# A two-layer HGRN2 and forgetting-attention trunk on one core: meta tokens turned first, a second PSUM bank for a head's outputs, half-tile parts stacked, key tiles that end with query tiles

## The chip, the core and the metric

The kernel runs on one NeuronCore of a Trainium2 chip. Its engines are TensorE (PE in the profile; PEld is its weight loads), VectorE (DVE), ScalarE (ACT), GpSimd (POOL) and SyncE (SP, which issues the DMAs). Each runs its own instructions in order and waits for others by semaphores. The metric is the device time of one execution in microseconds (us); lower is better.

## The reference

A sequence of 16 meta tokens and 1024 real ones, 1024 features wide, goes through two layers. The first mixes by a gated linear recurrence, the second by forgetting attention; each is followed by a feed-forward net with a causal convolution of width 3.

```python
# layer 0: per head (8 heads, 128 wide), chunks of 64 tokens, the meta tokens one chunk of 16
S_t = diag(f_t) S_{t-1} + k_t v_t^T ;  o_t = S_t^T q_t
o = RMSNorm_per_head(o) * head_gain * silu(g) ;  mix = o @ w_out
# layer 1: per head (16 heads, 64 wide), causal, one shared k, v and decay sum c
p = softmax(q k^T / 8 + c_q - c_k) ;  o = p @ v ;  mix = o @ w_out
# after each: h += RMSNorm(mix), then
u = causal_conv3(RMSNorm(h) @ w_up)          # 2 x 2752 columns
h += RMSNorm((silu(gate) * val) @ w_down)    # 2752 rows
```

## The kernel before

Features lie on partitions, tokens on the free axis, in three blocks of 342 or 356 tokens. Matrix products are made from operands split in a high and a low part: `mm3s` (L137) issues three matmuls for each 128 rows of contraction, wh by xh (L141), wh by xl (L142) and wl by xh (L143). Weights come by `Weights.cols` and `Weights.rows`: a DMA into a raw tile, ACT's cast into wh, DVE's subtraction into wl (`split`, L96). PSUM tiles have tags with a fixed number of buffers: pj 2, g 3, pd 2, po 1.

*FFN* (`ffn`, L591). 2752 hidden features are 21 tiles of 128 and one half tile of 64. `tile_up` makes a tile's hidden values hh and hl. `downs` adds a chunk of three or four tiles into 8 accumulators, three blocks each. The half tile is in the first chunk, with two full ones: its high and low parts lie in two tiles, 64 rows each, and its three matmuls contract 64 rows.

*Recurrence* (`recurrence`, L438). For each head it turns values and key parts by PE transposes (`turn`, L448: two groups of four 128x128 blocks, then the meta tokens at L457, whose 16 rows ACT copies into mt), makes the scores, the start state from the meta tokens (L490), the state products (L496) and the outputs (L516, L518), four blocks per PSUM tile po, which ACT evacuates twice, copy and square (L505, L506). `weave` (L248) mixes this stream on PE with the next head's input projections by columns yielded, and PE's order there is written out by that, not by the scheduler.

*Attention* (L750 on). Queries go in tiles of 114, three to a block. `score_steps` makes a query tile's logits and softmax in a tile L, of a width kn that ends with the query tile. `sum_steps` turns L in key tiles of 128 (L899), copies each into pTh and pTl, and adds v by pTh (L911) and v by pTl (L912) into po. The keys are 1040 wide, so the last key tile, which only the third block of a head reads, has 16 rows. The values are turned to key rows by `turn` (L789), in three steps per head pair: 2, 3 and 3 key tiles and the tail of 16, each copied by ACT (L805, L809) and subtracted by DVE (L806, L810). POOL clears the part of L between kn and the end of its key tile (L864). `weave` mixes the heads with the next pairs' projections. Outside of these two woven stretches a scheduler orders all engines.

Of the kernel before, what the change touches and what calls it, by code (L numbers as in the profile page):

```python
# [12 lines left out]
U32 = mybir.dt.uint32  # L13
# [42 lines left out]
def tile_yoco(ctx: ExitStack, tc: tile.TileContext, hT, gains, lbl, w_in, head_g, w_oa,  # L56
# [23 lines left out]
    def f(ap):  # L80
        return ap.bitcast(F32)
# [18 lines left out]
    class Weights:  # L100
# [28 lines left out]
            return lambda kt: (wh[:, kt * P:(kt + 1) * P], wl[:, kt * P:(kt + 1) * P])  # L129

        def rows(self, w, r0, n=P, name="w"):
            raw, wh, wl = self.load(lambda raw: [(raw[:n, :D], w[r0:r0 + n, :])], name)
            with tc.high_priority(offset=self.offset):
                split(wh[:n, :D], wl[:n, :D], raw[:n, :D])
            return lambda ot: (wh[:n, ot * P:(ot + 1) * P], wl[:n, ot * P:(ot + 1) * P])

    def mm3s(pt, pairs, sl):  # L137

        n = len(pairs)
        for j, ((wh, wl), (xh, xl)) in enumerate(pairs):  # L140
            PE.matmul(pt, wh, xh[:, sl], start=(j == 0), stop=False)  # L141
            PE.matmul(pt, wh, xl[:, sl], start=False, stop=False)  # L142
            PE.matmul(pt, wl, xh[:, sl], start=False, stop=(j == n - 1))  # L143
            yield 3 * pt.shape[-1]

    def mm3(pt, pairs, sl):
        for _ in mm3s(pt, pairs, sl):
# [290 lines left out]
    def recurrence(h):  # L438
# [8 lines left out]

        def turn(src, dst, j):  # L448

            for b4 in range(2):  # L450
                pt = psum("g")
                for j4 in range(4):
                    PE.transpose(pt[:, j4 * P:(j4 + 1) * P], src[:, pr(4 * b4 + j4)], ident)
                A.copy(dst[:, 4 * b4:4 * b4 + 4].rearrange("p j v -> p (j v)"), pt)
                yield 8 * P
            pm = psum("g")
            PE.transpose(pm[:, :P], src[:, :P], ident)  # L457
            A.copy(mt[:NMETA, j], pm[:NMETA, :P])
            yield 2 * P


        decay = sm.tile([P, 3, NPAIR], F32, tag="decay", name=nm("decay"))
# [47 lines left out]
        evacuate(slice(0, NMETA), pm[:, :NMETA])  # L510
        yield 4 * NMETA
        for b4 in range(2):
            po = psum("po")
            for j in range(4 * b4, 4 * b4 + 4):
                oc = slice(j % 4 * P, (j % 4 + 1) * P)
                PE.matmul(po[:, oc], vt[:, j], atv[:, j], start=True, stop=False)  # L516
                yield 4 * P
                PE.matmul(po[:, oc], S[:, j], qi[:, pr(j)], start=False, stop=True)  # L518
                yield 4 * P
            evacuate(slice(NMETA + 512 * b4, NMETA + 512 * b4 + 512), po)  # L520
# [70 lines left out]
    def ffn(l, blocks, x, r, WW, hid, accu, done, then=None):  # L591
# [21 lines left out]

        def tile_up(j):
            c0, m = HID[j]
            hh, hl = (unit(i, f"h{j}", F32R) for i in hid[count["hid"] % len(hid)])
            count["hid"] += 1
            ws = [WW.cols(w_up[l], [c0]), WW.cols(w_up[l], [DFF + c0])] if m == P else [WW.cols(w_up[l], [c0, DFF + c0])]
            halo = [None, None]

            def block(t0, n):
                sl, y = slice(t0, t0 + n), []
                for i, w in enumerate(ws):
                    if i:
                        yield
                    pt = psum("pj")[:, :n]
                    mm3(pt, [(w(kt), x[kt]) for kt in range(KT)], sl)
                    with tc.high_priority(offset=OFF):
                        yi, halo[i] = conv(pt, j + i * FT, halo[i], sl)
                    y.append(yi)  # L630
                if m < P:
                    y.append(tmp("y", n))
                    A.copy(y[1][:m], y[0][m:2 * m])
                yg, yv = y[0][:m], y[1][:m]
                A.activation(yg, yg, AF.Silu)
                V.tensor_mul(yv, yv, yg)
                split(hh[:m, sl], hl[:m, sl], yv)
                yield

            return (hh[:m], hl[:m]), block  # L640

        def first(b):
            if not ups:
# [109 lines left out]
    NG = 2 * KT * NB  # L753
    lo, hi = slice(0, HD), slice(HD, P)
    WA = Weights([30, 31], [(37, 41), (42, 43), (39, 44)])
    pair = [dict() for _ in range(KT)]
    head_ = [dict() for _ in range(2 * KT)]
    seen = set()
# [30 lines left out]
    def turn(hp, i):  # L789

        p = pair[hp]
        if i == 0:
            p["vs"] = [unit(VS[hp % 2][j], f"vs{j}", F32R)[:, :D].rearrange("p (k c) -> p k c", c=P) for j in range(2)]
            p["tail"] = tmp("res", 2 * P, F32R)[:NMETA].rearrange("p (k c) -> p k c", c=P)
        ks = [(0, 1), (2, 3, 4), (5, 6, 7)][i]
        vT = p["v"][1]
        pt = psum("g")
        for j, k in enumerate(ks):
            PE.transpose(pt[:, j * P:(j + 1) * P], vT[:, k * P:(k + 1) * P], ident)
        if i == 2:  # L800
            PE.transpose(pt[:NMETA, 3 * P:], vT[:, SEQ:], ident)
        p3 = pt.rearrange("p (k c) -> p k c", c=HD)
        for j in range(2):
            d, q = p["vs"][j][:, ks[0]:ks[-1] + 1], p3[:, j:2 * len(ks):2]
            A.copy(d[:, :, :HD], q)  # L805
            V.tensor_sub(d[:, :, HD:], q, f(d[:, :, :HD]))  # L806
        if i == 2:
            d, q = p["tail"], p3[:NMETA, 6:]
            A.copy(d[:, :, :HD], q)  # L809
            V.tensor_sub(d[:, :, HD:], q, f(d[:, :, :HD]))  # L810
        seen.add(("turn", hp, i))

    def halves(n, i):
# [20 lines left out]
    def dense():  # L834
        for hp in range(1, KT):
            for i in range(NB):
                yield from project("v", hp, i)
                if i:
                    turn(hp, i - 1)
                    yield 3 * P  # L840
            for i in range(NB):
                yield from project("k", hp, i)
                if i == 0:
                    turn(hp, 2)
                    yield 4 * P
                yield from project("q", hp, i)
        while ("split", 2 * KT - 1, NB - 1) not in seen:
            yield None
        yield from one()

    def score_steps(s):


        n, g = divmod(s, NB)
        h, g0 = head_[n], BLK_B[g][0]
        out = h[g] = []
        for i in range(3):
            q0 = g0 + i * QT
            kn = q0 + QT
            L = unit(rot("p", PU), "L")  # L860
            c4 = sm.tile([P, 8], F32, tag="c4", name=nm("c4"), bufs=4)[:QT]
            pad = min(T, -(-kn // P) * P)
            if pad > kn:
                G.memset(L[:QT, kn:pad], 0.0)  # L864
            pcs = pieces(kn)
            for x, (a, b) in enumerate(pcs):
                pt = psum("pd")[:QT, :b - a]
                last = x == len(pcs) - 1
                PE.matmul(pt, h["q"][0][:, q0:q0 + QT], h["k"][:, a:b], start=True, stop=False)
                PE.matmul(pt, h["q"][1][:, q0:q0 + QT], h["k"][:, a:b], start=False, stop=not last)  # L870
                if last:
                    PE.matmul(pt[:, b - a - QT:], identb[:QT], maskb[:QT], start=False, stop=True)
                with tc.high_priority(offset=OFF):
                    V.tensor_tensor_reduce(L[:QT, a:b], pt, h["c"][:QT, a:b], 1.0, 3e38 if x == 0 else c4[:, x - 1:x],
                                           ALU.add, ALU.min, c4[:, x:x + 1])
                if last:
                    A.activation(L[:QT, :kn], L[:QT, :kn], AF.Exp, scale=-1.0, bias=c4[:, x:x + 1], accum_out=c4[:, 5:6])
                    V.reciprocal(c4[:, 6:7], c4[:, 5:6])
                    V.tensor_scalar(L[:QT, :kn], L[:QT, :kn], c4[:, 6:7], None, ALU.mult)
                    out.append((L, kn))  # L880
                yield 2 * (b - a) + last * QT

    def sum_steps(s):
# [2 lines left out]
        g0, gn = BLK_B[g]  # L886
        pu = head_[n][g]
        p, j = pair[n // 2], n % 2
        nk = -(-pu[-1][1] // P)
        av = psum("po")  # L890
        pT = {}

        def turned(kt):
            c0 = rot("pt", [0, gn, 2 * gn])
            kw = min(P, T - kt * P)
            f0 = min(i for i in range(3) if kt * P < pu[i][1])
            pt = psum("g")
            for i in range(f0, 3):
                PE.transpose(pt[:kw, i * QT:(i + 1) * QT], pu[i][0][:QT, kt * P:kt * P + kw], ident[:QT, :QT])  # L899
# [7 lines left out]

        def summed(kt):
            th, tl, ts = pT[kt]
            v = p["vs"][j][:, kt] if th.shape[0] == P else p["tail"][:, j]  # L910
# [57 lines left out]
            yield SLACK  # L968

    def list_steps(s):  # L970
        nk = -(-(BLK_B[s % NB][0] + 3 * QT) // P)
        return sum_steps(s), 4 * 3 * QT * nk

    o_last = []
    B0 = BLK_B[0][0]
# [91 lines left out]
```

## Time and profile before

| | |
|---|---|
| median of 3 runs | 2924.54 us (2918.55 to 2925.66) |
| profiled execution | 2919.62 us, span 2917.9 us |
| PE busy | 2796.7 us, 96% |
| DVE, ACT, POOL busy | 1819.5, 1258.1, 389.8 us |
| moved by DMA | 162.64 MB, 56 GB/s on average |

Busy is the time in which an engine has an instruction under way; for PE the ends of matmuls are modelled and overlap, so the starts in a timeline say more. The waits of PEld show when the next weight load could have begun and did not.

### The profile page before, as it was taken

The page shows a single profiled execution, that of the slowest core. Times are in us where ns is not written, and L with a number is a line of the kernel's source. Part 1 is how long each engine was busy: PE and PEld are TensorE (multiplying, and loading weights), DVE is VectorE, ACT ScalarE, POOL GpSimd, SP SyncE. Part 2 cuts the span into 40 slices and gives each one's busy share as a digit, 9 for nine tenths or more (in the row PEclk, how much of TensorE's full clock was granted, in tenths as well). Part 3 has the DMA queues.
Part 4 walks back from the last instruction along what each step waited for, and adds up shares of the span by engine and source line. Part 5 has one row for each costly group of instructions (what it writes and reads, how often), then busy time and mean ns, then how long its engine had stood idle before and what let it go on. Part 6 is the DMA issues. An engine that isn't in the chain of part 4 may idle for free. (4 is left out here: it accounts for less than half of the span.)

```text
span 2917.9 us, 45973 instructions
## 1 busy us (share of the span) xinstructions
PE 2796.7 (96%) x17754; PEld 2711.2 (93%) x17754; DVE 1819.5 (62%) x3713; ACT 1258.1 (43%) x2399; POOL 389.8 (13%) x851
## 2 busy tenths in 40 slices
PE   8999999999999999999799999998989999999997
PEld 8899999888999999999789898898988999999997
DVE  5545444276555655656878888887683655565566
ACT  6444445445322322323466666666564322232232
POOL 2000000042000100103511111100140100010012
PEclk9999999999999999999899999999999999999999
DMA  4111111132111111111311111112241111111103
GB/s 131 29 37 30 37 37 44 44 102 78 51 44 37 52 51 51 44 51 45 107 49 44 45 45 45 45 44 94 66 122 58 44 51 44 37 53 49 51 30 111
DMA packets 202763, 162.64 MB, mean 56 GB/s; under 512 B 13952, under 2 KB 194096, under 8 KB 202544
## 3 DMA queue, kind: packets, MB, share of 16 engines
q1 hardware_dynamic: 202544, 159.70, 18.7%
q8 instruction: 139, 2.28, 0.3%
q14 instruction: 80, 0.66, 0.1%
HBM read 139.01 MB, written 20.66 MB: 55 GB/s over the span
## 5 line engine op out<-in xcount | busy, mean ns | idle before, releaser
L141 PE MATMUL pj<-x,wh 128*128 128x342 f32 (+1 forms) x2640 | 871.3, 330 | 11.8 <-DVE z L731 6.1
L143 PE MATMUL pj<-x,wl 128*128 128x342 f32 (+1 forms) x2640 | 848.8, 321 | 1.7 <-DVE wl L98 1.7
L142 PE MATMUL pj<-x,wh 128*128 128x342 f32 (+1 forms) x2640 | 848.5, 321 | 0.0
L141 PEld LDWEIGHTS pj<-x,wh 128*128 128x128 f32 x2640 | 500.4, 190 | 19.0 <-ACT sq L181 5.9
L143 PEld LDWEIGHTS pj<-x,wl 128*128 128x128 f32 x2640 | 499.3, 189 | 2.0 <-DVE wl L98 2.0
L142 PEld LDWEIGHTS pj<-x,wh 128*128 128x128 f32 x2640 | 500.8, 190 | 0.2
L97 ACT CAST wh<-raw 128x1024 fp32r<-128x1024 f32 (+1 forms) x202 | 208.5, 1044 | 348.4 <-PE g L142 281.9
L141 PE MATMUL g<-h,wh 128*128 128x342 f32 (+2 forms) x1056 | 347.5, 331 | 0.1
L98 DVE TENSOR_TENSOR wl<-raw,wh 128x1024 fp32r<-128x1024 f32 (+1 forms) x202 | 255.8, 1274 | 141.8 <-ACT wh L97 116.9
L142 PE MATMUL g<-h,wh 128*128 128x342 f32 (+2 forms) x1056 | 338.9, 322 | 0.0
L143 PE MATMUL g<-h,wl 128*128 128x342 f32 (+2 forms) x1056 | 338.0, 321 | 0.0
L141 PE MATMUL pj<-hnh,wh 128*128 128x356 f32 (+1 forms) x720 | 261.6, 363 | 9.6 <-ACT wh L97 7.3
L669 DVE TENSOR_TENSOR acc<-acc,g 128x342 f32<-128x342 f32 (+1 forms) x288 | 147.2, 512 | 193.6 <-PE g L143 193.4
L143 PE MATMUL pj<-hnh,wl 128*128 128x356 f32 (+1 forms) x720 | 233.2, 324 | 0.8 <-DVE wl L98 0.8
L142 PE MATMUL pj<-hnl,wh 128*128 128x356 f32 (+1 forms) x720 | 232.9, 323 | 0.0
L606 ACT ACTIVATE y<-u,cw 128x342 f32<-128x342 f32 (+1 forms) x258 | 150.6, 584 | 181.2 <-DVE u L601 173.6
L607 DVE SCALAR_TENSOR_TENSOR y<-u,cw,y 128x342 f32<-128x342 f32 (+1 forms) x258 | 149.5, 579 | 114.5 <-ACT y L606 114.3
L141 PEld LDWEIGHTS g<-h,wh 128*128 128x128 f32 (+1 forms) x1056 | 198.4, 189 | 20.4 <-issue 18.7
L182 POOL TENSOR_TENSOR acc<-acc,sq 128x342 f32<-128x342 f32 (+1 forms) x162 | 170.9, 1061 | 302.5 <-ACT sq L181 272.3
L601 DVE TENSOR_TENSOR u<-pj,r 128x342 f32<-128x342 f32 (+1 forms) x258 | 132.6, 514 | 118.2 <-PE pj L143 113.8
L142 PEld LDWEIGHTS g<-h,wh 128*128 128x128 f32 (+1 forms) x1056 | 199.5, 189 | 1.3 <-issue 0.8
L143 PEld LDWEIGHTS g<-h,wl 128*128 128x128 f32 (+1 forms) x1056 | 199.3, 189 | 0.4 <-issue 0.4
(231 smaller groups left out, 4804.5 us busy)
## 6 DMA issues: line engine op xcount, KB each, us to landing
raw<-in_w_up_dram SPq DMA_DIRECT2D x84, 512.0 KB, 4.0
raw<-in_w_dn_dram SPq DMA_DIRECT2D x42, 512.0 KB, 4.5
raw<-in_w_in_dram SPq DMA_DIRECT2D x32, 512.0 KB, 4.1
raw<-in_kv_w_dram SPq DMA_DIRECT2D x16, 512.0 KB, 4.1
res<-h SPq DMA_DIRECT2D x44, 171.0 KB, 2.7
h<-mix SPq DMA_DIRECT2D x40, 171.0 KB, 2.1
cn<-csum SPq DMA_DIRECT2D x32, 171.0 KB, 3.7
raw<-in_w_oa_dram SPq DMA_DIRECT2D x8, 512.0 KB, 3.5
```

The source lines that it names most:

```text
L97: A.copy(hi, src)
L98: V.tensor_sub(lo, src, f(hi))
L141: PE.matmul(pt, wh, xh[:, sl], start=(j == 0), stop=False)
L142: PE.matmul(pt, wh, xl[:, sl], start=False, stop=False)
L143: PE.matmul(pt, wl, xh[:, sl], start=False, stop=(j == n - 1))
L182: eng.tensor_add(acc, acc, sq)
L601: V.tensor_mul(u[:, 2:], pt, r()[:, sl])
L606: A.activation(y, u[:, 2:], AF.Copy, scale=cw[:, j, 2:3])
L607: V.scalar_tensor_tensor(y, u[:, 1:n + 1], cw[:, j, 1:2], y, ALU.mult, ALU.add)
L669: V.tensor_add(acc_u[ot][:, sl], acc_u[ot][:, sl], pt)
```

## The change

Four edits. (1) The half tile's high and low parts lie under each other in one tile of 128 rows; its rows of w_down are loaded twice, one copy under the other, and the lower half of wl is cleared on POOL. `mm3s` then issues two matmuls for it instead of three. (2) `turn` of the recurrence turns the meta tokens before the two groups of blocks. (3) The second half of a head's outputs takes a PSUM tile of tag g instead of po. (4) Key tile 0 has 128 keys, the other eight 114, so that they end where query tiles end; the tile L is no longer cleared, the values are turned to the same tiles (rows 114 to 127 of the first tile by a copy and a subtraction of their own, since the others have 114), and the tail becomes a tile of 114 rows.

```diff
@@ Weights.rows
-            raw, wh, wl = self.load(lambda raw: [(raw[:n, :D], w[r0:r0 + n, :])], name)
+            raw, wh, wl = self.load(lambda raw: [(raw[i:i + n, :D], w[r0:r0 + n, :]) for i in range(0, P, n)], name)
...
-                split(wh[:n, :D], wl[:n, :D], raw[:n, :D])
...
+                A.copy(wh[:, :D], raw[:, :D])
+                if n < P:
+                    G.memset(wl[n:, :D].bitcast(U32), 0)
+                V.tensor_sub(wl[:n, :D], raw[:n, :D], f(wh[:n, :D]))
@@ mm3s
-            PE.matmul(pt, wh, xl[:, sl], start=False, stop=False)
+            if xl is not None:
+                PE.matmul(pt, wh, xl[:, sl], start=False, stop=False)
@@ recurrence
+            pm = psum("g")
+            PE.transpose(pm[:, :P], src[:, :P], ident)
+            A.copy(mt[:NMETA, j], pm[:NMETA, :P])
+            yield 2 * P
             for b4 in range(2):
...
-            pm = psum("g")
-            PE.transpose(pm[:, :P], src[:, :P], ident)
-            A.copy(mt[:NMETA, j], pm[:NMETA, :P])
-            yield 2 * P
...
-            po = psum("po")
+            po = psum(("po", "g")[b4])
@@ ffn, block
-                split(hh[:m, sl], hl[:m, sl], yv)
+                if m == P:
+                    split(hh[:, sl], hl[:, sl], yv)
+                else:
+                    A.copy(hh[:m, sl], yv)
+                    V.tensor_sub(hh[m:, sl], yv, f(hh[:m, sl]))
@@ attention
+    KEYS = [(0, BLK_B[0][0] + QT)] + [(BLK_B[0][0] + k * QT, QT) for k in range(1, NQ)]
...
         for j in range(2):
...
+            parts = [(p["vs"][j][:QT, 3 * i:3 * i + n], p3[:QT, j:2 * n:2])]
+            if i == 0:
+                parts.append((p["vs"][j][96:, :1], p3[96:, j:j + 1]))
+            elif i == 2:
+                parts.append((p["tail"][:QT, j:j + 1], p3[:QT, 4 + j:5 + j]))
+            for d, q in parts:
+                A.copy(d[:, :, :HD], q)
+                V.tensor_sub(d[:, :, HD:], q, f(d[:, :, :HD]))
...
-                    yield 3 * P
+                    yield 6 * P
...
-                    yield 4 * P
+                    yield 6 * P
...
-            if pad > kn:
-                G.memset(L[:QT, kn:pad], 0.0)
...
-        nk = -(-pu[-1][1] // P)
+        nk = 3 * g + 3
...
-            kw = min(P, T - kt * P)
-            f0 = min(i for i in range(3) if kt * P < pu[i][1])
+            k0, kw = KEYS[kt]
+            f0 = max(0, kt - 3 * g)
```

In PE's order before, one group of the first down projection of layer 0: g is the PSUM tile; h_733 and h_734, h_741 and h_742 are the high and low parts of the two full tiles, h_749 and h_750 those of the half tile.

```order
L141 MATMUL g_6268<-h_733_5420,wh_6137 128x342
L142 MATMUL g_6268<-h_734_5421,wh_6137 128x342
L143 MATMUL g_6268<-h_733_5420,wl_6138 128x342
L141 MATMUL g_6268<-h_741_5434,wh_6143 128x342
L142 MATMUL g_6268<-h_742_5435,wh_6143 128x342
L143 MATMUL g_6268<-h_741_5434,wl_6144 128x342
L141 MATMUL g_6268<-h_749_5448,wh_6149 128x342
L142 MATMUL g_6268<-h_750_5449,wh_6149 128x342
L143 MATMUL g_6268<-h_749_5448,wl_6150 128x342
```

The same group in PE's order now (L145, L148 and L149 are the former L141, L142 and L143):

```order
L145 MATMUL g_6269<-h_733_5420,wh_6136 128x342
L148 MATMUL g_6269<-h_734_5421,wh_6136 128x342
L149 MATMUL g_6269<-h_733_5420,wl_6137 128x342
L145 MATMUL g_6269<-h_741_5434,wh_6142 128x342
L148 MATMUL g_6269<-h_742_5435,wh_6142 128x342
L149 MATMUL g_6269<-h_741_5434,wl_6143 128x342
L145 MATMUL g_6269<-h_749_5448,wh_6148 128x342
L149 MATMUL g_6269<-h_749_5448,wl_6149 128x342
```

The half tile has two matmuls instead of three, and h_750 is gone.

In PE's order before, the recurrence of the second head where its key parts are turned: d is what is turned, mt holds the meta tokens' turned rows, and hnh, hnl, wh, wl belong to the woven projection of the next head.

```order
L453 MATMUL g_1352<-ident,d_932 128x128 x4
L141 MATMUL pj_1324<-hnh_15_94,wh_1213 128x342
L142 MATMUL pj_1324<-hnl_16_95,wh_1213 128x342
L143 MATMUL pj_1324<-hnh_15_94,wl_1214 128x342
L141 MATMUL pj_1380<-hnh_1_80,wh_1375 128x356
L142 MATMUL pj_1380<-hnl_2_81,wh_1375 128x356
L143 MATMUL pj_1380<-hnh_1_80,wl_1376 128x356
L457 MATMUL g_1384<-ident,d_932 128x128
L490 MATMUL g_1387<-mt 128x128
```

The same place now (L463 is the former L453, L496 the former L490):

```order
L463 MATMUL g_1346<-ident,d_932 128x128 x4
L145 MATMUL pj_1324<-hnh_13_92,wh_1213 128x342
L148 MATMUL pj_1324<-hnl_14_93,wh_1213 128x342
L149 MATMUL pj_1324<-hnh_13_92,wl_1214 128x342
L145 MATMUL pj_1324<-hnh_15_94,wh_1213 128x342
L148 MATMUL pj_1324<-hnl_16_95,wh_1213 128x342
L149 MATMUL pj_1324<-hnh_15_94,wl_1214 128x342
L463 MATMUL g_1358<-ident,d_932 128x128 x4
L145 MATMUL pj_1383<-hnh_1_80,wh_1378 128x356
L148 MATMUL pj_1383<-hnl_2_81,wh_1378 128x356
L149 MATMUL pj_1383<-hnh_1_80,wl_1379 128x356
L496 MATMUL g_1387<-mt 128x128
```

The meta tokens' transpose has moved ahead of these rows, and three dense matmuls stand between the last turned blocks and the reader of mt.

In ACT's order before, the same place of the third head: kt is the copy of four turned blocks, mt that of the meta tokens.

```order
L454 COPY kt_1726<-g_1843 128x512
L454 COPY kt_1726<-g_1855 128x512
L97 CAST wh_2128<-raw_2127 128x1024
L361 ACTIVATE s_1776<-s_1776 128x342
L458 COPY mt<-g_1887 16x128
```

And now (L464 is the former L454, L367 the former L361):

```order
L458 COPY mt<-g_1843 16x128
L464 COPY kt_1726<-g_1849 128x512
L97 CAST wh_2128<-raw_2127 128x1024
L464 COPY kt_1726<-g_1861 128x512
L367 ACTIVATE s_1776<-s_1776 128x342
```

The copy of mt now stands first, and the second copy of kt has come to stand behind the weight cast.

## Rows read from the trace of the kernel before

**Rows 1.** The page, part 1: busy time, share of the span, instructions.

```profile
PE 2796.7 (96%) x17754; PEld 2711.2 (93%) x17754; DVE 1819.5 (62%) x3713; ACT 1258.1 (43%) x2399; POOL 389.8 (13%) x851
```

**Rows 2.** Windows: stretch, its us, busy PE PEld DVE ACT POOL (count), clock, DMA.

```profile
702.58:746.15 43.57, 43.57 (x218) 33.23 (x216) 5.74 (x12) 15.16 (x33) 0.85 (x4) 1.00 0.09 25
1490.00:2076.00 586.00, 561.02 (x3738) 526.28 (x3738) 474.79 (x1324) 368.64 (x891) 48.62 (x124) 0.99 0.17 48
```

**Rows 3.** Timeline of PE, down projection: start, duration, line, out<-in, rows*columns.

```profile
704.33 0.42 PE L141 MATMUL g<-h,wh 128*128 128x342 f32 x1
704.59 0.32 PE L142 MATMUL g<-h,wh 128*128 128x342 f32 x1
...
705.22 0.32 PE L143 MATMUL g<-h,wl 128*128 128x342 f32 x1
705.47 0.42 PE L141 MATMUL g<-h,wh 64*128 64x342 f32 x1
705.73 0.32 PE L142 MATMUL g<-h,wh 64*128 64x342 f32 x1
705.88 0.32 PE L143 MATMUL g<-h,wl 64*128 64x342 f32 x1
706.13 0.43 PE L141 MATMUL g<-h,wh 128*128 128x342 f32 x1
```

**Rows 4.** Line L336, a clear on POOL: ns min/median/max, starts, form.

```profile
L336 POOL MEMSET at<- x1: 968/968/968, 1.7 to 1.7; 128x1040 f32 x1
```

**Rows 5.** Waits of PEld, whole span: us in total, times, longest.

```profile
PEld po L912 <- DVE pTl L904: 19.1, 35, 1.5
...
PEld g L490 <- ACT mt L458: 10.4, 8, 1.8
...
PEld po L516 <- ACT sq L506: 8.0, 8, 1.1
```

**Rows 6.** Timeline of PE, recurrence of the third head.

```profile
213.67 0.27 PE L457 MATMUL g<-ident,d 128*128 128x128 f32 x1
215.02 0.49 PE L490 MATMUL g<-mt 128*128 128x128 f32 x2 [1.07 <-ACT mt L458]
```

**Rows 7.** Timeline of ACT at the same place.

```profile
212.91 0.59 ACT L454 COPY kt<-g 128x512 f32<-128x512 f32 x1 [0.79 <-PE g L453]
213.39 1.05 ACT L97 CAST wh<-raw 128x1024 fp32r<-128x1024 f32 x1
214.34 0.49 ACT L361 ACTIVATE s<-s 128x342 f32<-128x342 f32 x1
214.73 0.24 ACT L458 COPY mt<-g 16x128 f32<-16x128 f32 x1
```

**Rows 8.** Timeline of PE, a last key tile of 16 rows.

```profile
1742.34 0.32 PE L143 MATMUL pj<-x,wl 128*128 128x342 f32 x1
1742.59 0.31 PE L911 MATMUL po<-pTh,res 16*128 16x114 f32 x1
1742.74 0.27 PE L912 MATMUL po<-pTl,res 16*128 16x114 f32 x1
1742.94 0.43 PE L141 MATMUL pj<-x,wh 128*128 128x342 f32 x1
```

**Rows 9.** Lines of PE by form, L899: count | busy us, mean ns | idle before.

```profile
L899 PE MATMUL g<-ident,L 114*128 114x114 f32 x704 | 116.4, 263 | 7.9 <-DVE L L879 5.0 <-DVE pTl L904 2.5
...
L899 PE MATMUL g<-ident,L 114*16 114x114 f32 x16 | 4.2, 262 | 0.1
```

**Rows 10.** Waits in attention (1495 to 2075).

```profile
ACT vs L805 <- DVE vs L806: 5.9, 9, 1.7
```

**Rows 11.** Line L810, the tail's subtraction.

```profile
L810 DVE TENSOR_TENSOR res<-g,res x8: 269/276/280, 1489.2 to 1951.1; 16x128 fp32r<-16x128 f32 x8
```

**Rows 12.** Timeline of PE, transposes of 114 rows ahead of 128-row matmuls.

```profile
1789.77 0.46 PE L899 MATMUL g<-ident,L 114*128 114x114 f32 x3
...
1790.23 0.32 PE L142 MATMUL pj<-x,wh 128*128 128x342 f32 x1
```

More of the change, by code (lines that the diff above doesn't have):

```diff
@@ L131, in rows @@
         def rows(self, w, r0, n=P, name="w"):
-            raw, wh, wl = self.load(lambda raw: [(raw[:n, :D], w[r0:r0 + n, :])], name)
+            raw, wh, wl = self.load(lambda raw: [(raw[i:i + n, :D], w[r0:r0 + n, :]) for i in range(0, P, n)], name)
             with tc.high_priority(offset=self.offset):
-                split(wh[:n, :D], wl[:n, :D], raw[:n, :D])
-            return lambda ot: (wh[:n, ot * P:(ot + 1) * P], wl[:n, ot * P:(ot + 1) * P])
+                A.copy(wh[:, :D], raw[:, :D])
+                if n < P:
+                    G.memset(wl[n:, :D].bitcast(U32), 0)
+                V.tensor_sub(wl[:n, :D], raw[:n, :D], f(wh[:n, :D]))
+            return lambda ot: (wh[:, ot * P:(ot + 1) * P], wl[:, ot * P:(ot + 1) * P])
     def mm3s(pt, pairs, sl):
@@ L141, in mm3s @@
             PE.matmul(pt, wh, xh[:, sl], start=(j == 0), stop=False)
-            PE.matmul(pt, wh, xl[:, sl], start=False, stop=False)
+            if xl is not None:
+                PE.matmul(pt, wh, xl[:, sl], start=False, stop=False)
             PE.matmul(pt, wl, xh[:, sl], start=False, stop=(j == n - 1))
-            yield 3 * pt.shape[-1]
+            yield (2 + (xl is not None)) * pt.shape[-1]
     def mm3(pt, pairs, sl):
@@ L615, in tile_up @@
             c0, m = HID[j]
-            hh, hl = (unit(i, f"h{j}", F32R) for i in hid[count["hid"] % len(hid)])
+            ua, ub = hid[count["hid"] % len(hid)]
+            hh, hl = unit(ua, f"h{j}", F32R), unit(ub, f"h{j}", F32R) if m == P else None
             count["hid"] += 1
@@ L636, in block @@
                 V.tensor_mul(yv, yv, yg)
-                split(hh[:m, sl], hl[:m, sl], yv)
+                if m == P:
[3 more added lines that the diff above has]
+                    V.tensor_sub(hh[m:, sl], yv, f(hh[:m, sl]))
                 yield
-            return (hh[:m], hl[:m]), block
+            return (hh, hl), block
         def first(b):
@@ L793, in turn @@
             p["vs"] = [unit(VS[hp % 2][j], f"vs{j}", F32R)[:, :D].rearrange("p (k c) -> p k c", c=P) for j in range(2)]
-            p["tail"] = tmp("res", 2 * P, F32R)[:NMETA].rearrange("p (k c) -> p k c", c=P)
-        ks = [(0, 1), (2, 3, 4), (5, 6, 7)][i]
+            p["tail"] = tmp("res", 2 * P, F32R).rearrange("p (k c) -> p k c", c=P)
         vT = p["v"][1]
         pt = psum("g")
[L798 to L801, printed above, removed]
+        for j, (k0, kw) in enumerate(KEYS[3 * i:3 * i + 3]):
+            PE.transpose(pt[:kw, j * P:(j + 1) * P], vT[:, k0:k0 + kw], ident)
         p3 = pt.rearrange("p (k c) -> p k c", c=HD)
+        n = 3 - i // 2
         for j in range(2):
[L804 to L810, printed above, removed]
+            parts = [(p["vs"][j][:QT, 3 * i:3 * i + n], p3[:QT, j:2 * n:2])]
[6 more added lines that the diff above has]
+                V.tensor_sub(d[:, :, HD:], q, f(d[:, :, :HD]))
         seen.add(("turn", hp, i))
@@ L861, in score_steps @@
             c4 = sm.tile([P, 8], F32, tag="c4", name=nm("c4"), bufs=4)[:QT]
-            pad = min(T, -(-kn // P) * P)
-            if pad > kn:
-                G.memset(L[:QT, kn:pad], 0.0)
             pcs = pieces(kn)
@@ L894, in turned @@
             c0 = rot("pt", [0, gn, 2 * gn])
-            kw = min(P, T - kt * P)
-            f0 = min(i for i in range(3) if kt * P < pu[i][1])
+            k0, kw = KEYS[kt]
+            f0 = max(0, kt - 3 * g)
             pt = psum("g")
             for i in range(f0, 3):
-                PE.transpose(pt[:kw, i * QT:(i + 1) * QT], pu[i][0][:QT, kt * P:kt * P + kw], ident[:QT, :QT])
+                PE.transpose(pt[:kw, i * QT:(i + 1) * QT], pu[i][0][:QT, k0:k0 + kw], ident[:QT, :QT])
             ts = slice(f0 * QT, gn)
@@ L909, in summed @@
             th, tl, ts = pT[kt]
-            v = p["vs"][j][:, kt] if th.shape[0] == P else p["tail"][:, j]
+            v = (p["vs"][j][:, kt] if kt < 8 else p["tail"][:, j])[:th.shape[0]]
             PE.matmul(av[:, ts], v, th[:, ts], start=(kt == 0), stop=False)
@@ L970, in list_steps @@
     def list_steps(s):
-        nk = -(-(BLK_B[s % NB][0] + 3 * QT) // P)
-        return sum_steps(s), 4 * 3 * QT * nk
+        return sum_steps(s), 4 * 3 * QT * 3 * (s % NB + 1)
     o_last = []
```

## The prediction, made before the changed kernel was run

> **What bounds the kernel now.** I read the page's first part first. TensorE (PE) is busy 96% of the span [rows 1], so a change can gain only by taking matmuls away, by closing the spaces between matmuls, or by ending one of the few waits of PE. For spaces I read the timeline of PE, where the start of a matmul minus the start of the one before it is its stride; for waits, the list of what the weight loads (PEld) waited for, because a weight load's idle time is real idle time, while a matmul's modelled end hides some of it. Three places matter, one for each part of the change: the first down projection of each FFN, which PE fills completely (43.57 of 43.57 us) [rows 2], the recurrence of the HGRN2 layer, and attention, where DVE is also near its limit (474.79 of 586 us, 81%; PE 561.02) [rows 2].
>
> **Part 1, the FFN half tile.** A group is one output tile by one token block: three hidden tiles, nine matmuls, and the third tile has only 64 rows. With 342 columns and 128 rows the plain stride is 0.158 us (704.59 to 705.22 is four strides) [rows 3]. Into the 64-row matmuls the stride is 0.25, the next 0.26, then 0.15, out again 0.25, and the first one after that 0.26 (704.33 to 704.59) [rows 3]. So a change between 128 and 64 rows costs some 0.19 us, twice per group, and the group takes 1.80 us (704.33 to 706.13) instead of nine plain strides, 1.42. After the change the high and low halves lie under each other in one tile of 128 rows: eight matmuls, all of 128 rows. Eight plain strides are 1.26 us, so a group gains 0.54. There are 8 output tiles x 3 blocks x 2 layers = 48 groups: **25.9 us**, of which 48 x 0.158 = 7.6 for the matmuls removed and 18.3 for the switches. The longer stretch agrees: 43.57 us for 24 groups [rows 2], against 24 x 8 x 0.158 = 30.3.
>
> The Trainium skill has two sentences that pull apart here. "TensorEngine Tiling (Array Packing)", Key Properties, says that a change of tiling mode drains TensorE; by that the switches cost something, and rows 3 agree, with 0.19 us each. "TensorE: Matmul & The Clock Gate", LDWEIGHTS, says that load time goes by columns and a 32-row load takes as long as a 128-row one; by that alone only the removed matmuls would count and the part would be worth 7.6 us. It is a rival below, though the trace is against it.
>
> What part 1 adds: the half tile's rows of w_down are fetched twice (one more DMA of 256 KB per layer), and POOL clears 64x1024 of wl. The nearest clear, 128x1040, took 0.97 us [rows 4]. In POOL's order it stands between two halo copies, while PE still has up projections left; behind it wait a halo copy, then DVE's convolution, then a PSUM buffer of the up projection. I cost it at nothing; without that cover it is at most 2 x 0.97 us. The cast of these weights covers 128 rows instead of 64, beside others, at the same number of columns. In ACT's order the casts of the next chunk's first two weight tiles stand ahead of the first copy out of the down projection, before and now, so a shorter one exposes none of them.
>
> **Part 2, the recurrence.** Two waits repeat in all eight heads: L490 waits for the copy mt, 10.4 us in total, and L516 for the square sq, 8.0 us [rows 5]. The first: the meta tokens are turned last (L457) and L490, which reads them, follows at once, 1.35 us later (213.67 to 215.02) [rows 6]. On ACT that copy stands behind a second turned block (212.91), a weight cast of 1.05 us and a tanh, and starts at 214.73 [rows 7]. Turned first, mt is copied before all of these, and L490 has nothing to wait for. What is late next is the copy of the second block kt, now behind the weight cast in ACT's order. It would end near 213.39 + 1.05 + 0.59 = 215.0 [rows 7]; its reader is the fifth of the L496 products. L490 now starts near 213.8, and between it and that reader stand fifteen dense matmuls and four products, over 2.4 us for the dense ones alone: after 216.2. So the wait goes and nothing takes its place, with about 1 us to spare. The second: both halves of a head's outputs used the one buffer of po, so L516 waited until both evacuations of the first half had read it. The second half now has a buffer of g; its previous user is the copy of kt, long read. The number of g buffers per head becomes 15, and the last norm (L527) takes the buffer of the second half, after the slack that the order already leaves there. Sum 10.4 + 8.0 = 18.4, and at the low end, if the L490 wait moves to L496, 8.0. I take **18 us**.
>
> **Part 3, attention.** The last key tile had 16 rows, once per head: 16 pairs of L911 and L912. Into the pair the stride is 0.25 instead of 0.158 (1742.34 to 1742.59), and the pair itself takes 0.35 (1742.59 to 1742.94) [rows 8]; after it I count 0.10 for the switch back, as in rows 3. With 114 rows the switches go, 0.19 together, and the two matmuls of 114 columns take between 114/342 of a plain stride each (0.11 together) and two full strides (0.32). The gain is 0.22 to 0.43 per pair, 3.5 to 6.9 us; since rows 8 look like drains rather than columns I take **6 us**. The number of transposes and their moving columns stay (114 for L899); only their weight columns go from 128, or 16, to 114. They took 263 ns with 128 and 262 with 16 [rows 9], so nothing is gained or lost. The clears of L on POOL go; PE is not seen to wait for them, so that is worth nothing.
>
> Against this, turning the values needs 3 more copies on ACT and 3 more subtractions on DVE per head pair, 24 of each. A 16x128 copy took 0.24 [rows 7] and a subtraction 0.28 us [rows 11]. The copy waits for the subtraction before it, as it did 9 times before for 5.9 us, 0.66 each [rows 10]. ACT's and DVE's work for pTh and pTl queues behind them, and PE waits for pTl already (19.1 us) [rows 5]. If all of that landed on PE it would be 24 x (0.24 + 0.28 + 0.66) = 28 us; if PE's lead covers it, nothing. The existing 48 copies (6 per head pair) had 5.9 / 48 = 0.12 us of wait each, so I take 24 x 0.12, **3 us lost**. The changed yields also reweave dense matmuls with scores in another order; a few us either way, none in the sum.
>
> **Sum.** 25.9 + 18 + 6 - 3 = 46.9 us. The profiled execution took 2919.62 us (span 2917.9), 4.9 below the median of 2924.54, and the runs lie between 2918.55 and 2925.66. From its own time the sum gives 2872.7, from the median 2877.6. I forecast **2876 us**.
>
> **The rivals.**
> - *Rows do not matter to PE.* Then part 1 gives 7.6 and part 3 no more than the columns: 7.6 + 18 - 3 = 22.6, **2902 us**. For it speaks only the rule above; rows 3 and 8 show the strides. 4%.
> - *The wait moves along.* ACT gives the kt copy as late as it gave mt, and L496 waits: 10.4 less, **2887 us**. For it: in ACT's new order the weight cast does stand before that copy. Against it: the 1 us to spare. 10%.
> - *Attention gives it back.* The longer chain of copies and subtractions holds pTh and pTl; up to 28 us instead of 3, so 2877 to 2902, say **2890 us**. For it: DVE's 81%. Against it: the values are turned well before they are summed. 12%.
> - *114 rows are a switch too: slower.* The change makes eight of nine key tiles 114 rows high among 128-row matmuls: 2 + 5 + 8 = 15 visits per head, 240 in all. At rows 3's two switches, 0.38 us per visit, it is 91 us; less the 40.9 that then remain (46.9 without part 3's 6), the time is **2975 us**. It decides from 40.9 / 240 = 0.17 us per visit on. Against it: three 114-row transposes and the 128-row L141 behind them took 0.46 us (1789.77 to 1790.23) [rows 12], no more than three times 0.10 and a plain stride. 2%. The Trainium skill, "TensorEngine Tiling (Array Packing)", Available Configurations, lists modes of 128, 64 and 32 rows and takes row tiling for contractions up to 64, so 114 goes with 128; rows 12 agree.
> - *It does not do what it says*, for instance since a few dearer places absorb all of it: within 0.3%. 2%.
>
> **How the numbers follow.** The forecast has 70%. Its own range is 2919.6 - 25.9 - 18.4 - 6.9 = 2868 without a loss, less some 6 us for waits that the new weave may close, to 2884 where attention gives back a little. For 8 in 10 it must reach through the moved wait (2887) and half of the attention rival: **2862 to 2892**. About 0.3% (9 us) is what a measurement of this kernel tells from no change. Faster by more: 0.95; same: 0.03; slower: 0.02.
>
> **What would show it.** In the profile after: the first down projections some 12.9 us shorter each, at an even stride of 0.158; L490 and the second L516 gone from PEld's waits, and no L496 in their place; the last pair of a head's sums without the 0.25 strides; PEld's waits for pTl and pTh near 19.1 and few us more. The prediction is wrong if L496 waits, if pTl's waits grow by more than 10 us, or if 114-row sums show strides of 0.25.

## The result, and the profile after

The changed kernel took 2879.51 us in the median of four runs (2877.34 to 2883.05), the kernel before 2923.72: a ratio of 0.9852 [0.9839, 0.9864], 43 us faster. The forecast was 2876. The changed kernel's profiled execution is its slowest run, 2883.05 us with a span of 2881.1.

The page's first part, in the columns of [rows 1]:

```profile
PE 2768.6 (96%) x17706; PEld 2709.2 (94%) x17706; DVE 1830.8 (64%) x3737; ACT 1258.2 (44%) x2421; POOL 369.6 (13%) x741
```

PE has 48 matmuls fewer and is as full as before. DVE has its 24 subtractions more, POOL its clears fewer.

**First down projection.** Two windows, which answer to [rows 2]: the first down projection of layer 0, and attention.

```profile
686.70:717.20 30.50, 30.50 (x192) 30.06 (x191) 4.58 (x8) 13.94 (x30) 0.38 (x3) 1.00 0.13 36
1459.50:2046.00 586.50, 557.28 (x3719) 525.65 (x3720) 483.91 (x1346) 372.66 (x914) 32.26 (x17) 0.98 0.17 48
```

The down projection has 192 matmuls instead of 216, and its window is 30.50 us long instead of 43.57; four of its matmuls now stand ahead of the window, before the last up projection (30.9 us with them). Attention is no shorter in this execution, at a granted clock of 0.98 where it was 0.99; the experiments show why that is not the whole story. One group of that down projection, in the timeline of PE, against [rows 3]:

```profile
700.65 0.32 PE L145 MATMUL g<-h,wh 128*128 128x342 f32 x1
...
701.44 0.32 PE L149 MATMUL g<-h,wl 128*128 128x342 f32 x1
701.60 0.32 PE L145 MATMUL g<-h,wh 128*128 128x342 f32 x1
701.76 0.32 PE L149 MATMUL g<-h,wl 128*128 128x342 f32 x1
701.92 0.33 PE L145 MATMUL g<-h,wh 128*128 128x356 f32 x1
```

Eight strides of 0.16, 1.27 us for the group where it was 1.80. The strides of 0.25 into and out of the half tile are gone.

**Recurrence.** The third head, where L463 turns key parts and L496 reads mt, in the timeline of PE, against [rows 6]:

```profile
208.83 0.60 PE L463 MATMUL g<-ident,d 128*128 128x128 f32 x4
209.18 0.41 PE L145 MATMUL pj<-hnh,wh 128*128 128x356 f32 x1
209.44 0.32 PE L148 MATMUL pj<-hnl,wh 128*128 128x356 f32 x1
209.59 0.33 PE L149 MATMUL pj<-hnh,wl 128*128 128x356 f32 x1
209.76 0.39 PE L496 MATMUL g<-mt 128*128 128x128 f32 x2
```

And the timeline of ACT there, against [rows 7]:

```profile
207.18 0.26 ACT L458 COPY mt<-g 16x128 f32<-16x128 f32 x1 [0.85 <-PE g L457]
208.09 0.59 ACT L464 COPY kt<-g 128x512 f32<-128x512 f32 x1 [0.65 <-PE g L463]
208.87 1.05 ACT L97 CAST wh<-raw 128x1024 fp32r<-128x1024 f32 x1 [0.19 <-PE pj L148]
209.82 0.58 ACT L464 COPY kt<-g 128x512 f32<-128x512 f32 x1
```

The copy of mt ends at 207.44, and its reader comes at 209.76 without a wait. The second copy of kt has moved behind the weight cast and ends at 210.40, as the prediction read it from ACT's order.

**Waits of PE.** The list of what weight loads waited for, against [rows 5]. The first two rows are of the whole span; the third is the only place where the recurrence waits for a copy of turned blocks:

```profile
PEld po L922 <- DVE pTl L914: 19.3, 28, 2.4
PEld po L921 <- ACT pTh L913: 6.7, 14, 1.0
...
PEld pd L502 <- ACT kt L464: 1.0, 1, 1.0
```

L496 (the former L490) and the second half of the outputs (the former L516) are not in the list. L502, the former L496, waits once in eight heads, for 1.0 us. The wait for pTl is 19.3 where it was 19.1.

**Tail of attention.** The last pair of a head's sums, now with 114 rows, in the timeline of PE, against [rows 8]:

```profile
1785.34 0.32 PE L149 MATMUL pj<-x,wl 128*128 128x342 f32 x1
1785.50 0.22 PE L921 MATMUL po<-pTh,res 114*128 114x114 f32 x1
1785.55 0.27 PE L922 MATMUL po<-pTl,res 114*128 114x114 f32 x1
1785.66 0.38 PE L145 MATMUL pj<-x,wh 128*128 128x342 f32 x1
1785.88 0.32 PE L148 MATMUL pj<-x,wh 128*128 128x342 f32 x1
```

From the matmul ahead of the pair to the second one behind it are 0.54 us (1785.34 to 1785.88). Before, the same four strides were 0.25 + 0.15 + 0.20 + 0.27 = 0.87; the row behind those of [rows 8] ends the last one:

```profile
1743.21 0.32 PE L142 MATMUL pj<-x,wh 128*128 128x342 f32 x1
```

Into the pair the stride is now the plain 0.16. Not all of the sixteen places are as clean, since PE waits in some of them, before and now: over all sixteen the four strides add up to 15.7 us before and 10.8 now.

### The profile page after: what moved, and what is told of

It is laid out like the page before. It is cut to its first block, busy times and chain, and to the rows that moved or that the text cites. A ratio compares the mean times of both kernels' runs of the same rounds, so it can differ in the third digit from the quotient of the medians.

```text
span 2881.1 us, 45581 instructions
## 1 busy us (share of the span) xinstructions
PE 2768.6 (96%) x17706; PEld 2709.2 (94%) x17706; DVE 1830.8 (64%) x3737; ACT 1258.2 (44%) x2421; POOL 369.6 (13%) x741
## 5 line engine op out<-in xcount | busy, mean ns | idle before, releaser
L145 PE MATMUL pj<-x,wh 128*128 128x342 f32 (+1 forms) x2640 | 871.1, 330 | 12.6 <-DVE u L607 6.3
L149 PE MATMUL pj<-x,wl 128*128 128x342 f32 (+1 forms) x2640 | 849.3, 322 | 2.8 <-DVE wl L98 2.8
L148 PE MATMUL pj<-x,wh 128*128 128x342 f32 (+1 forms) x2640 | 849.3, 322 | 0.0
L145 PEld LDWEIGHTS pj<-x,wh 128*128 128x128 f32 x2640 | 500.8, 190 | 18.9 <-DVE u L607 7.2
L149 PEld LDWEIGHTS pj<-x,wl 128*128 128x128 f32 x2640 | 499.9, 189 | 3.1 <-DVE wl L98 3.1
L148 PEld LDWEIGHTS pj<-x,wh 128*128 128x128 f32 x2640 | 501.5, 190 | 0.1
L145 PE MATMUL g<-h,wh 128*128 128x342 f32 (+1 forms) x1056 | 339.0, 323 | 0.3
L149 PE MATMUL g<-h,wl 128*128 128x342 f32 (+1 forms) x1056 | 337.7, 321 | 0.4 <-DVE wl L138 0.4
L148 PE MATMUL g<-h,wh 128*128 128x342 f32 (+1 forms) x1008 | 323.8, 322 | 0.0
L97 ACT CAST wh<-raw 128x1024 fp32r<-128x1024 f32 x142 | 146.0, 1045 | 341.6 <-PE g L148 282.1
L145 PE MATMUL pj<-hnh,wh 128*128 128x356 f32 (+1 forms) x720 | 261.8, 364 | 9.3 <-ACT wh L97 7.0
L98 DVE TENSOR_TENSOR wl<-raw,wh 128x1024 fp32r<-128x1024 f32 x142 | 180.6, 1281 | 87.1 <-ACT wh L97 76.3
L149 PE MATMUL pj<-hnh,wl 128*128 128x356 f32 (+1 forms) x720 | 233.1, 324 | 0.8 <-DVE wl L98 0.8
L148 PE MATMUL pj<-hnl,wh 128*128 128x356 f32 (+1 forms) x720 | 232.8, 323 | 0.0
L145 PEld LDWEIGHTS g<-h,wh 128*128 128x128 f32 x1056 | 198.7, 189 | 2.5 <-ACT h L97 0.6
L149 PEld LDWEIGHTS g<-h,wl 128*128 128x128 f32 x1056 | 199.4, 189 | 0.6 <-DVE wl L138 0.6
L148 PEld LDWEIGHTS g<-h,wh 128*128 128x128 f32 x1008 | 190.6, 189 | 0.7 <-DVE h L98 0.2
```

Source lines behind the costliest of these rows:

```text
L97: A.copy(hi, src)
L98: V.tensor_sub(lo, src, f(hi))
```

## The experiments

All ratios are against the kernel before, run on the same chip. "Alone" means: the kernel before, with that edit only. The length of a stage is the difference of two starts in the timeline of PE.

### The half tile: rows and matmuls apart

The stacked half tile alone, edit 1 of the change with all its lines; its core:

```diff
-            PE.matmul(pt, wh, xl[:, sl], start=False, stop=False)
+            if xl is not None:
+                PE.matmul(pt, wh, xl[:, sl], start=False, stop=False)
...
+                    A.copy(hh[:m, sl], yv)
+                    V.tensor_sub(hh[m:, sl], yv, f(hh[:m, sl]))
```

> Only the stacked half tile; recurrence and attention as before. If a change between 64 and 128 rows costs PE 0.19 us each time, the gain is 48 groups x 0.54 = 25.9 us, each first down projection 12.9 us shorter. If rows do not matter to PE, 48 x 0.158 = 7.6 us. Changed kernel's trace: from the recurrence's end to the end of the first down projection 9.6 us were gained in layer 0 and 6.6 from the end of attention on in layer 1, 3.3 and 6.3 less than 12.9. If the new order of the stage ahead of the down projection, which the stacked tile brings, eats these, they are missing here too and the gain is 16 to 17 us; if the changed attention brings them, layer 1 shows the full 12.9 here.

Measured: 2897.83 us, ratio 0.9927 [0.9907, 0.9946], 21 us less. The second kernel keeps all three matmuls and only makes them 128 rows high, by rows that hold zeros:

```diff
-                split(wh[:n, :D], wl[:n, :D], raw[:n, :D])
-            return lambda ot: (wh[:n, ot * P:(ot + 1) * P], wl[:n, ot * P:(ot + 1) * P])
+                split(wh[:, :D], wl[:, :D], raw[:, :D])
+            return lambda ot: (wh[:, ot * P:(ot + 1) * P], wl[:, ot * P:(ot + 1) * P])
...
+            if m < P:
+                G.memset(hh[m:].bitcast(U32), 0)
+                G.memset(hl[m:].bitcast(U32), 0)
```

> The half tile keeps its three matmuls, but all of 128 rows: the lower 64 rows of both parts are zero, and the weights' rows are loaded twice. No matmul is removed, only the switches go. If switches cost 0.38 us per group, the gain is 48 x 0.38 = 18.3 us; if rows do not matter to PE, nothing, or a loss by the clears on POOL.

Measured: 2906.61 us, 0.9958 [0.9941, 0.9974], 12 us less with the same number of matmuls. Its timeline of PE in the first down projection, the last matmul of the full tiles, the three of the half tile (715.65 to 715.96) and the first of the next group:

```profile
715.49 0.32 PE L143 MATMUL g<-h,wl 128*128 128x342 f32 x1
715.65 0.32 PE L141 MATMUL g<-h,wh 128*128 128x342 f32 x1
715.80 0.32 PE L142 MATMUL g<-h,wh 128*128 128x342 f32 x1
715.96 0.32 PE L143 MATMUL g<-h,wl 128*128 128x342 f32 x1
716.12 0.32 PE L141 MATMUL g<-h,wh 128*128 128x356 f32 x1
```

All nine strides of this group are 0.16, 1.43 us in all, with nothing computed less: what cost time was the change of rows. The strides of all matmuls of the first down projections, added up:

| us | layer 0 | layer 1 | both |
|---|---|---|---|
| before | 43.6 | 43.4 | 87.0 |
| rows alone, three matmuls | 34.8 | 36.6 | 71.4 |
| stacked, two matmuls | 30.9 | 32.9 | 63.8 |

The rows are worth 15.6 us and the removed matmuls 7.6, together 23.2. The last row is the same for this edit alone and for the whole change. The ratios, 21 us for the stacked half tile (16 to 27 by its interval) and 12 for the rows alone (8 to 17), agree with these sums; read at one clock, below, they are 21 and 15. The 2 us that layer 1's down projection takes longer than layer 0's in the last two rows are no stride. The timeline of PE of the changed kernel shows them:

```profile
2171.17 0.32 PE L148 MATMUL g<-h,wh 128*128 128x342 f32 x1
2171.84 0.57 PE L149 MATMUL g<-h,wl 128*128 128x342 f32 x2 [0.35 <-DVE wl L138]
...
2173.83 0.42 PE L145 MATMUL pj<-x,wh 128*128 128x342 f32 x1 [1.42 <-DVE u L607]
```

The scheduler has pulled the full tiles of two groups of the down projection (tile g) ahead of the last up projection (pj). They wait for a weight's low part, which DVE makes late, and then the up projection waits for its PSUM buffer, 1.42 us. Before, all groups stood behind it.

### The recurrence: one edit, the other, and both

Edits 2 and 3 of the change together, without the others:

> Meta tokens turned first and the second half of the outputs in g, nothing else. If both waits go and nothing takes their place: 18.4 us gained, the last L518 some 18 us earlier, no L496 among PEld's waits but one of at most 1 us. If the wait for mt moves to the kt copy: 8 us. If the mixer stage behind it loses by its order alone, the gain at the end is less than at the last L518.

Then edit 2 alone, the meta tokens turned first:

```diff
+            pm = psum("g")
+            PE.transpose(pm[:, :P], src[:, :P], ident)
+            A.copy(mt[:NMETA, j], pm[:NMETA, :P])
+            yield 2 * P
             for b4 in range(2):
...
-            pm = psum("g")
-            PE.transpose(pm[:, :P], src[:, :P], ident)
-            A.copy(mt[:NMETA, j], pm[:NMETA, :P])
-            yield 2 * P
```

> Only the meta tokens turned first. If the prediction's term is right, 10.4 us gained and L490 gone from the waits, while L516 still waits for sq with 8 us. If the recurrence's gain came from the buffer, nothing.

And edit 3 alone, the second bank:

```diff
-            po = psum("po")
+            po = psum(("po", "g")[b4])
```

> Only the second half of a head's outputs in a g buffer. If the prediction's term is right, 8.0 us gained and L516 gone from the waits, L490 still there with 10.4. If po's buffer and the copy hide each other, the two gains alone sum to less or more than the 17 of both.

Measured, the medians being 2903.74, 2917.68 and 2915.32 us:

| | ratio | 95% | gain | first matmul to last L518 |
|---|---|---|---|---|
| before | 1 | | | 529.5 us |
| meta tokens first, alone | 0.9989 | 0.9978 to 1.0 | 3 us | 523.7 |
| second bank, alone | 0.9978 | 0.9968 to 0.9988 | 6 us | 525.2 |
| both | 0.9943 | 0.9923 to 0.9964 | 17 us | 512.2 |
| whole change | 0.9852 | 0.9839 to 0.9864 | 43 us | 510.6 |

The end of the stage can be read from the row of its last output line (durations in ns, then first and last start): before, meta tokens first, second bank, both.

```profile
L518 PE MATMUL po<-qi,S x128: 270/273/275, 112.1 to 536.9; 128*128 128x128 f32 x128
```

```profile
L518 PE MATMUL po<-qi,S x128: 270/273/275, 112.1 to 530.8; 128*128 128x128 f32 x128
```

```profile
L518 PE MATMUL g<-qi,S x64: 270/272/275, 118.2 to 532.4; 128*128 128x128 f32 x64
```

```profile
L518 PE MATMUL g<-qi,S x64: 270/273/275, 117.3 to 519.4; 128*128 128x128 f32 x64
```

By these lengths the two edits give 5.8 and 4.3 us of this stage alone, 10.1 together, but 17.3 when both are made. The lengths hold different shares of the lower TensorE clock, though: in this stage PE stood at it for 6.8 us before, and for 6.8, 17.1 and 10.2 us in the three. The five heads from the third to the seventh, from the last L518 of the second to that of the seventh, ran at the full clock in all four. As windows, in the same order (behind the five engines' busy times stands the granted clock):

```profile
170.91:476.68 305.77, 296.89 (x1983) 290.43 (x1982) 136.51 (x235) 136.44 (x200) 14.04 (x15) 1.00 0.12 35
```

```profile
169.79:472.92 303.13, 295.46 (x1983) 290.50 (x1982) 137.02 (x235) 135.95 (x200) 14.05 (x15) 1.00 0.12 36
```

```profile
172.76:473.48 300.72, 295.35 (x1982) 290.31 (x1981) 136.58 (x235) 136.60 (x200) 14.08 (x15) 1.00 0.12 36
```

```profile
168.65:462.67 294.02, 294.02 (x1982) 290.48 (x1981) 137.00 (x235) 135.78 (x200) 14.07 (x15) 1.00 0.13 37
```

A head takes 61.15, 60.63, 60.14 and 58.80 us there. The meta tokens alone gain 0.53 per head, the second bank alone 1.01 and both 2.35, which is 4.2, 8.1 and 18.8 us in eight heads. So the second bank alone is worth the 8.0 us of its wait, and the meta tokens alone are not worth the 10.4 of theirs; 6.5 of the 18.8 us come only when both edits are made.

With the meta tokens first, L490's wait of 10.4 us is gone, and the weight loads' list has this at its head:

```profile
PEld po L516 <- ACT sq L506: 13.0, 8, 1.8
```

It was 8.0. With the second bank alone, L516 is gone from the list, and the first wait stands as it stood:

```profile
PEld g L490 <- ACT mt L458: 10.3, 8, 1.8
```

Why L516 waits longer in the first of them is to be seen on ACT. Its timeline in the third head, meta tokens first alone; L396 to L398 are the exponentials of the next head's gates, L505 and L506 the evacuations of po:

```profile
221.89 1.07 ACT L397 ACTIVATE b<-b 128x1040 f32<-128x1040 f32 x1
222.87 1.06 ACT L398 ACTIVATE d<-d 128x1040 f32<-128x1040 f32 x1
223.83 0.48 ACT L369 ACTIVATE y<-sg 128x356 f32<-128x356 f32 x1
224.22 0.56 ACT L505 COPY o<-po 128x512 f32<-128x512 f32 x1
224.69 0.60 ACT L506 ACTIVATE sq<-po 128x512 f32<-128x512 f32 x1
```

And the timeline of PE there:

```profile
222.95 0.38 PE L518 MATMUL po<-qi,S 128*128 128x128 f32 x2
...
225.34 0.49 PE L516 MATMUL po<-at,vt 128*128 128x128 f32 x2 [1.54 <-ACT sq L506]
```

PE has written the first half at 222.95 + 0.38 = 223.3, but ACT reaches the copy at 224.22, since the exponentials and an activation (L369) stand ahead of it in its order. They come earlier than in the kernel before, but by less than PE does: L397 starts 1.2 us earlier (223.10 before), PE's L518 2.5 us earlier. In the kernel before, the timeline of ACT there reads:

```profile
225.85 0.59 ACT L505 COPY o<-po 128x512 f32<-128x512 f32 x1 [0.32 <-PE po L518]
```

ACT had been idle for 0.32 us and took the copy as soon as L518 had written. So the time that PE won at L490 it lost in part at L516, whose wait grew by 5.0 us, and only with the second bank does it keep it. In both kernels with both edits neither wait is listed, and the stage is 17.3 and 18.9 us shorter.

### Attention: alone, and with fewer copies

Edit 4 alone, all lines of the change's attention; its core:

```diff
-            kw = min(P, T - kt * P)
-            f0 = min(i for i in range(3) if kt * P < pu[i][1])
+            k0, kw = KEYS[kt]
+            f0 = max(0, kt - 3 * g)
```

> Key tiles of 128 and 8 x 114, nothing else. By the prediction's terms 6 us gained at the tails less 3 for the 24 more copies and subtractions: 3 us faster. By the changed kernel's trace, in which attention took 1.0 us longer: 0 to 2 us slower in attention, so that copies and the other weave cost 7 or so. If the changed attention also disturbs the mixer stage behind it, another 3 to 6 us slower.

Measured: 2916.33 us, 0.9983 [0.9972, 0.9993], 5 us less. Its waits for pTl and pTh in the weight loads' list:

```profile
PEld po L910 <- DVE pTl L902: 17.3, 26, 2.4
...
PEld po L909 <- ACT pTh L901: 7.3, 15, 1.0
```

Then the same without the extra copy and subtraction for rows 114 to 127 of the first key tile; this kernel leaves these 14 keys out of the sums:

```diff
-            if i == 0:
-                parts.append((p["vs"][j][96:, :1], p3[96:, j:j + 1]))
-            elif i == 2:
+            if i == 2:
...
-            PE.matmul(av[:, ts], v, th[:, ts], start=(kt == 0), stop=False)
-            PE.matmul(av[:, ts], v, tl[:, ts], start=False, stop=(kt == nk - 1))
+            PE.matmul(av[:, ts], v[:QT], th[:QT, ts], start=(kt == 0), stop=False)
+            PE.matmul(av[:, ts], v[:QT], tl[:QT, ts], start=False, stop=(kt == nk - 1))
```

> As the attention change alone, but rows 114 to 127 of the first key tile are left out of the values and of the sums (so 14 keys are missing from the output): 16 copies on ACT and 16 subtractions on DVE fewer. The attention change alone took 581.5 us in attention against 585.1 before. If the extra copies cost PE time, as the prediction had it with 3 us for 24 pairs, 2 us more are gained here; if they cost up to 1.18 us a pair, 19 us; if PE's lead covers them, nothing beyond the scatter of some 3 us.

Measured: 2917.01 us, 0.9984 [0.9973, 0.9996]: 16 copies and 16 subtractions fewer change nothing that can be measured. Attention, from the first transpose of L to the last sum, took 581.5 and 580.5 us in these two. Over all profiled executions, the six with the old attention had 585.1 to 588.1 (mean 586.9), the four with the new one 580.5 to 586.1 (mean 582.5). So the stage gained about 4 us, and the profile after, with 586.1, has the longest of the four.

Part of this is work that has left the stage. Of the output projection's matmuls (tiles oh and ol), 258 stand ahead of the last sum in the six and 237 in the four: the changed yields moved 21 of them behind it, 3.3 us at a stride of 0.158. They are not lost again there. The 60 us behind the last sum, in the kernel before and in the one with attention alone:

```profile
2075.88:2135.88 60.00, 55.18 (x341) 53.03 (x342) 36.21 (x71) 26.40 (x55) 24.45 (x25) 0.97 0.34 100
```

```profile
2072.88:2132.88 60.00, 56.70 (x356) 55.31 (x355) 35.22 (x69) 26.60 (x55) 24.53 (x25) 0.97 0.34 101
```

At the same granted clock PE gets 15 matmuls more into these 60 us, where it waited before. The last matmul of the projection starts 63.3 us behind the last sum instead of 62.3, so 2.3 of the 3.3 us are gained. With the tails' 4.9 this makes some 7 us for this part.

### The whole again

The changed kernel once more, beside those of the second comparison:

> The whole change once more. If the 169.1 us from the end of attention to the end of layer 1's first down projection and the 586.1 us of attention belong to the one execution with its half clock, this profile shows some 166 to 167 and 582 to 584; if they belong to the order of the whole kernel, 169 and 586 again. Time 2876 to 2883.

Measured: 2880.6 us, 0.9856 [0.9836, 0.9876]. The parts alone gained 21 + 17 + 5 = 43 us, the whole 42 here and 43 in the first comparison. They add up, though the intervals of the parts (6, 6 and 3 us to either side) would hide a few us given back between them. Attention took 582.0 us in this profile, so the 586.1 belonged to the one execution. From the last sum to the end of layer 1's first down projection it took 168.2, between the two values expected, with PE at the lower clock for 13.7 us of it; in the profile after it was 10.2.

### The same runs at one clock

A run's time follows the mean clock that TensorE was granted in it. Of the kernel before, runs with 0.982 took 2922.62 to 2927.08 us, those with 0.986 and 0.987 took 2913.13 to 2915.36. A straight line with one slope for all kernels and a height for each, through all 98 runs of these comparisons, has 2.0 us per 0.001 and leaves 1.7 us of scatter. Read at 0.983:

| | us | gain | runs |
|---|---|---|---|
| before | 2922.8 | | 38 |
| half tile stacked | 2901.6 | 21 | 4 |
| half tile, rows alone | 2907.7 | 15 | 4 |
| recurrence, both | 2904.4 | 18 | 4 |
| meta tokens first | 2918.3 | 4.5 | 10 |
| second bank | 2915.2 | 7.5 | 10 |
| attention | 2914.8 | 8 | 10 |
| attention, fewer copies | 2915.0 | 8 | 10 |
| whole change | 2878.2 | 45 | 8 |

This takes the clock as given from outside. The two attention kernels had 0.983 and 0.982 on average, the kernel before 0.984; if the change itself lowers the clock, the ratios above are the truer price. For attention the profiled executions speak for that: PE stood at the lower clock in this stage for 21.6 to 28.2 us in the four with the new attention and for 14.1 to 20.6 in the six with the old one. Why is not shown. The order of the three parts, and that the copies cost nothing that can be measured, hold either way: ten runs each and 1.7 us of scatter would have told a difference of some 1.5 us between the two attention kernels, and 2 were expected. That the two recurrence edits gain more together (18) than apart (4.5 + 7.5) agrees with the heads at the full clock.

## Why the prediction was right, step by step

The sum was 46.9 us and 42 to 43 came. The forecast of 2876 stood 3.5 us below the median.

- **The half tile, 25.9 predicted.** 23.2 came in the first down projections. The removed matmuls gave the 7.6 of the sum exactly. The switches gave 15.6 instead of 18.3, and that is the term that was too large: 2.0 of the 2.7 missing are the waits in layer 1, where the scheduler set matmuls of the down projection ahead of the last up projection. The prediction had looked at layer 0's stretch and doubled it. Layer 0 alone gave 12.7, against 12.95.
- **What part 1 adds, predicted at nothing.** The up projections ahead of it, from the last L518 in layer 0 and from the last sum in layer 1, took 166.8 and 133.5 us with this edit alone, 2.0 more in both layers than before (165.7 and 132.5). The five other kernels whose FFN is that of the kernel before had 162.3 to 165.7 and 132.1 to 135.2 there, so this difference is not told from scatter. In the two executions of the whole it was 4.2 and 6.7, with PE at the lower clock for 6.8 us more than before in these stages, worth about half that by the strides at the end of this document. A cost of the additions is not shown, and one of a few us is not excluded.
- **The recurrence, 18 predicted.** It took 18.9 us less in the profile after, 17.3 with this part alone, and 18.8 by the heads at the full clock. But the prediction counted 10.4 and 8.0 as two separate prices, and only the second is one: alone, by the same heads, the edits gave 4.2 and 8.1. It asked what would be late next at L490 and looked at kt, which waited once, for 1.0 us; it did not ask the same of L516, where 5.0 of the 10.4 us go when the second bank is missing. The sum held because both were in the change; for the meta tokens alone its price would have been 6 us too large.
- **The tails, 6 predicted.** A clean pair gave 0.33 us, and all sixteen 4.9 together (15.7 to 10.8).
- **The copies, 3 lost predicted.** None is seen: the wait for pTl stayed (19.3), and taking away two thirds of the extra pairs changed nothing. So the net of 3 that the prediction gave attention was 5 by the ratio and 8 at one clock; the 2.3 us that the moved output projection filled into waits stood in its sum as none.

Of the rivals, *rows do not matter to PE* fell by the second kernel: 15.6 us for rows that hold zeros. The Trainium skill, "TensorEngine Tiling (Array Packing)", Key Properties, which says that a mode change drains TensorE, agrees with that; "TensorE: Matmul & The Clock Gate", LDWEIGHTS, which counts columns and not rows, describes the strides inside a run of one height and not those between two. *114 rows are a switch too* fell by the 0.16 us stride into a 114-row pair. *The wait moves along* came true once in eight heads, at 1.0 us instead of 10.4. *Attention gives it back* fell: its waits hardly grew, for pTl from 19.1 to 19.3 us, for pTh from 6.2 to 6.7. What the prediction did not see is the loss in layer 1's order and that the price of the meta tokens' edit hangs on the second bank.

## What to carry to other kernels

A remainder tile of 64 rows inside a run of 128-row matmuls costs two switches besides its own matmuls; stacking two operands of it to 128 rows, or filling it with zeros, takes both away, and the zeros alone gave two thirds of the gain here. Before two waits on one engine are added up as two gains, ask for each what the engine meets when it comes there earlier: other engines keep their own order and pace, and a later wait can grow by part of what the first gave, here by 5.0 of 10.4 us. Costing a stretch in one layer and multiplying by the layers is right for strides, not for the places where a scheduler joins two stages.

## What the runs showed of the hardware

A change between 128 and 64 rows cost 0.18 us: 43.6 less 34.8 in layer 0, for 48 changes. The four strides around a pair of 16 rows took 0.33 us more than those around the same pair of 114 rows, and into 114 rows from 128 the stride was the plain 0.16.

TensorE's clock is not fixed by the program. Two windows of the same stretch of the recurrence, the kernel with attention alone first, then the kernel before; behind the five engines' busy times stands the granted clock:

```profile
137.00:145.00 8.00, 6.68 (x28) 6.30 (x29) 1.62 (x3) 3.15 (x6) 0.00 (x0) 0.57 0.00 0
```

```profile
137.00:145.00 8.00, 6.78 (x51) 6.73 (x51) 2.35 (x4) 3.09 (x7) 0.00 (x0) 1.00 0.00 0
```

The code of this stage is the same in both, and PE had been idle at the same three places just before (0.62, 1.93 and 1.10 us in the one, 0.62, 1.93 and 1.22 in the other). In one the clock then fell to the lower level, 1.2 GHz, for some 7 us, in the other it stayed at 2.4 GHz. What decides it stays open. Where the clock was at the lower level, a projection's matmul of 356 columns had a stride of 0.30 us, and 0.16 right behind it (kernel before, 68.3 to 71.0 and 71.6 to 72.6). Over a run it adds up: of the changed kernel's second set the run with a mean clock of 0.985 took 2872.53 us, the three with 0.981 took 2879.77 to 2882.22. A part worth 5 us is therefore better compared by ten runs, at one clock, or over a stretch that ran at the full clock in both kernels, than by two whole profiles: the second bank's 8 us looked like 4.3 in one.
